# The first weight block of a streaming encoder layer: its two pieces loaded as two halves of 64 rows each, its cast shared by two engines, fewer warming matmuls

## The chip, the cores and the metric

The kernel runs on one core of a Trainium2 chip (trn2). The metric is the device time of one execution in microseconds (us), as the median of several runs. Before the change three runs gave 428.34, 428.74 and 429.11 us, median 428.74. The engines are named as the profile names them: PE (TensorE; PEld is its weight load), ACT (ScalarE), DVE (VectorE), POOL (GpSimd) and SP (SyncE, which here only issues DMAs).

## The reference

One inference step of an encoder layer for 256 prompt frames and 32 sample frames (288 together, `T`), width 1024. What matters here is its first step, one combined input projection of all frames in float32:

```python
def project(x, w_in, b_gates):
    B, T, _ = x.shape
    p = x @ w_in
    cuts = [int(c) for c in np.cumsum(COL_SIZES)[:-1]]
    (qa, ka, va, oa, za, ia, fa, qb, kb, vb, zb, qi, ki, wi, ga, gb) = jnp.split(p, cuts, axis=-1)
...
```

The pieces feed two branches (a gated matrix memory and a sparse attention), whose outputs are gated, projected again by `w_out_a`, `w_out_b` and `w_o`, added to the input and normalised.

## The kernel before

All weights are cut into tiles of 128 output columns by 1024 rows (8 blocks `k` of 128 rows), and a list `ORDER`, written out by hand, sets the order in which PE multiplies them. float32 accuracy is had from three products of a faster type: a weight `w` is split into a high part `wh` (a cast, on ACT) and the rest `wl = w - wh` (a subtraction, on DVE), the input likewise into `xh` and `xl`, and PE adds up `wh*xh`, `wh*xl` and `wl*xh` in PSUM.

For most tiles one DMA brings the whole tile. The first five tiles (`FIRST = 5`) are done in another way, so that PE can start early. The host packs for each of the 8 blocks `k` the block of the input (288 columns) and the block's share of the five tiles (5 x 128 columns) side by side in `in_first`, 928 columns in all (`LEAD`). Each block is loaded into a buffer `lead[k]` (`wst_k` in the trace), split by ACT and DVE, and multiplied for all five tiles at once by `first_products` (L957) into five PSUM banks.

Only block 0 comes in two pieces, the cut being at column 416 (`cut = T + 128`): piece A, the input and tile 0, is loaded from SP's queue (L163), and piece B, tiles 1 to 4, from ACT's queue (L164). SP then issues the DMAs of blocks 1 to 7 (L166). The work on a block is

```python
        act.copy(xh[:, k], raw[:, 0:T])                                              # L171
        if k == 0:
            dve.tensor_copy(wh[:, 0:128], raw[:, T:cut])                             # L173
        dve.tensor_tensor(xl[:, k], raw[:, 0:T], xh[:, k].bitcast(F32), OP.subtract) # L174
```

then, for block 0, `wl` of tile 0 on DVE (L176), and for every block the cast of the other `wh` columns on ACT (L178) and their `wl` on DVE (L179). ACT and DVE work through their instructions in the order written.

PE's first instructions are `WARM = 18` matmuls on a tile of zeros (`warm`, 256 columns, `keep_warm`, L150) whose result nobody reads. Behind them stands `first_products`: for block 0 the three products of tile 0 (288 columns each), then twelve of tiles 1 to 4 (224 columns each); for each later block fifteen products. From L896 to L898 on follow the other tiles. The order of instructions is fixed in the source (a manual schedule); a framework adds the semaphores, and an ACT table load (`ACT_TABLE_LOAD`) ahead of ACT's first operation that needs one.

Of the kernel before, what the change touches and what calls it, by code (L numbers as in the profile page):

```python
# [10 lines left out]
F32 = mybir.dt.float32  # L11
# [3 lines left out]
OP = mybir.AluOpType  # L15
# [7 lines left out]
T = TP + TS  # L23
# [2 lines left out]
BH, BD = 8, 128  # L26
IH, ID = 8, 64
CHUNK = 64
WARM = 18
MID = 4  # L30
FIRST = 5
LEAD = T + 128 * FIRST
# [53 lines left out]
def body(ctx, tc, a, o):  # L86
    nc = tc.nc
    pe, act, dve, pool, sp = nc.tensor, nc.scalar, nc.vector, nc.gpsimd, nc.sync
# [5 lines left out]
    def sb(name, shape, dt=F32, tag=None, bufs=1):  # L94
        return P.tile(shape, dt, name=name, tag=tag or name, bufs=bufs)
# [27 lines left out]
    def pair(name):  # L123
        return (sb(f"wh{name}", [128, KT * 128], F32R, tag="wh", bufs=4),
                sb(f"wl{name}", [128, KT * 128], F32R, tag="wl", bufs=4))
# [16 lines left out]
    xh = sb("xh", [128, KT, T], F32R)  # L142
    xl = sb("xl", [128, KT, T], F32R)
# [4 lines left out]
    def keep_warm(n):  # L148
        for _ in range(n):
            pe.matmul(wp[:, :256], lhsT=warm[:, :128], rhs=warm, start=True, stop=True)  # L150

    keep_warm(WARM)

# [6 lines left out]
    rtab = early2[:8, NREL:2 * NREL]  # L160
    lead = [sb(f"wst_k{k}", [128, KT * 128], tag="wst", bufs=8) for k in range(KT)]
    cut = T + 128
    sp.dma_start(lead[0][:, 0:cut], a["first"][:, 0, 0:cut])  # L163
    act.dma_start(lead[0][:, cut:LEAD], a["first"][:, 0, cut:])  # L164
    for k in range(1, KT):
        sp.dma_start(lead[k][:, 0:LEAD], a["first"][:, k])  # L166
    leads = []
    for k in range(KT):
        raw, (wh, wl) = lead[k], pair(f"_k{k}")
        leads.append((wh, wl))  # L170
        act.copy(xh[:, k], raw[:, 0:T])  # L171
        if k == 0:
            dve.tensor_copy(wh[:, 0:128], raw[:, T:cut])  # L173
        dve.tensor_tensor(xl[:, k], raw[:, 0:T], xh[:, k].bitcast(F32), OP.subtract)  # L174
        if k == 0:
            dve.tensor_tensor(wl[:, 0:128], raw[:, T:cut], wh[:, 0:128].bitcast(F32), OP.subtract)  # L176
        p = cut if k == 0 else T
        act.copy(wh[:, p - T:LEAD - T], raw[:, p:LEAD])  # L178
        dve.tensor_tensor(wl[:, p - T:LEAD - T], raw[:, p:LEAD], wh[:, p - T:LEAD - T].bitcast(F32), OP.subtract)  # L179
    for t in range(FIRST, FIRST + 3):  # L180
        load_tile(t)
# [763 lines left out]
    def out_bank(t):  # L945
        if t < FIRST:
            return bank(f"pj{t}")
        return ps.tile([128, 512], F32, name=f"pj{t}", tag="proj", bufs=2)

    def first_products():  # L950
        p = [out_bank(t) for t in range(FIRST)]
        for k, (wh, wl) in enumerate(leads):
            for tiles in ((0,), (1, 2, 3, 4)) if k == 0 else (range(FIRST),):
                for w, x in ((wh, xh), (wh, xl), (wl, xh)):
                    for t in tiles:
                        new = slice(CHUNK if ORDER[t][0] == "qi" else 0, T)
                        pe.matmul(p[t][:, new], lhsT=w[:, 128 * t:128 * t + 128], rhs=x[:, k, new],  # L957
                                  start=(k == 0 and w is wh and x is xh), stop=(k == KT - 1 and w is wl))
        return p


# [109 lines left out]
    def free_from(i):  # L1071
        n, j = ORDER[i - 8]
        return POS[n, j | 3] if n in ("vb", "va") else 0

    first = first_products()
    for t in (FIRST, FIRST + 1):
        split_hi(t)
# [117 lines left out]
```

## Time and profile before

| | before |
|---|---|
| median of 3 runs | 428.74 us (428.34 to 429.11) |
| the profiled execution, its own time | 429.2 us |
| its span, first to last instruction | 427.1 us |
| PE busy | 420.4 us, 98% of the span |
| first product of real data on PE | 5.07 us |
| end of block 0 on PE | 7.62 us |
| end of block 7 on PE | 19.79 us |

The profiled execution lies 0.46 us above the median, and its span 2.1 us below its own time. Times in the rows below count from the start of the span. A busy PE is not a PE at its full pace, since matmuls overlap: the start of one matmul to the start of the next is what one costs.

### The profile page before, as it was taken

To read this page: it belongs to the slowest core of one execution; us is meant where nothing else is said; L and a number is where in the kernel's file an instruction comes from. 1 tells how busy PE (TensorE), PEld (TensorE's weight loads), DVE (VectorE), ACT (ScalarE), POOL (GpSimd) and SP (SyncE) were. 2 spreads that over 40 slices of the span, in tenths; PEclk is the share of its full clock that TensorE was granted. 3 is DMA by queue.
4 is the path that set the end of the run, shared out by engine and by line. 5 is a ranking of instruction groups with operands and counts; after the bars stand their busy time and mean duration, and the time that the engine had idled before them with its cause. 6 is when DMAs were issued, how large, how long until landed. Compare 5 with 4: busy or idle time off the path is not lost.

```text
span 427.1 us, 8153 instructions
## 1 busy us (share of the span) xinstructions
PE 420.4 (98%) x3189; PEld 395.6 (93%) x3189; DVE 299.0 (70%) x601; ACT 226.7 (53%) x443; POOL 22.6 (5%) x41
## 2 busy tenths in 40 slices
PE   8999999999999999999999999999999999999994
PEld 7999999878999998789999999999999999998874
DVE  5669989986756665665999987876454465665674
ACT  6776445425666666458795465555434444446402
POOL 0000000000400000000001101101000000000031
PEclk9999999999999999999999999999999999999999
DMA  8987869575945630349544456545555658543014
GB/s 305 362 319 206 294 204 309 214 198 204 411 156 147 218 122 0 114 141 335 152 148 150 109 171 215 148 148 151 168 178 155 176 163 265 153 137 124 27 46 140
DMA packets 29746, 78.81 MB, mean 185 GB/s; under 512 B 8548, under 2 KB 11852, under 8 KB 28908
## 3 DMA queue, kind: packets, MB, share of 16 engines
q1 hardware_dynamic: 28844, 76.98, 56.0%
q10 hardware_dynamic: 864, 1.32, 0.9%
q8 instruction: 25, 0.41, 0.4%
q14 instruction: 13, 0.11, 0.1%
HBM read 72.52 MB, written 7.67 MB: 188 GB/s over the span
## 4 chain that ended last, share of the span: by engine, by line
PE 96%; DVE 1%; ACT 1%; POOLq 0%; issue 0%; DVEq 0%; ACTq 0%
PE pj L896 22%; PE pj L897 22%; PE pj L898 21%; PE yn L938 5%; PE pj L957 3%; PE pj L912 2%; PE pj L914 2%; PE pj L913 2%; PE warm_p L150 1%; PE vap L912 1%; PE vbp L912 1%; PE vbp L914 1%; PE vap L920 1%; PE vbp L920 1%; PE vap L914 1%; PE vbp L913 1%
## 5 line engine op out<-in xcount | busy, mean ns | idle before, releaser
L132 ACT CAST wh<-wst 128x1024 fp32r<-128x1024 f32 x112 | 117.8, 1052 | 137.5 <-PE pj L897 64.8
L896 PE MATMUL pj<-xh,wh 128*128 128x288 f32 x576 | 171.7, 298 | 0.1
L897 PE MATMUL pj<-xl,wh 128*128 128x288 f32 x576 | 169.9, 295 | 0.0
L898 PE MATMUL pj<-xh,wl 128*128 128x288 f32 x576 | 169.8, 295 | 0.0
L139 DVE TENSOR_TENSOR wl<-wst,wh 128x1024 fp32r<-128x1024 f32 x112 | 136.3, 1219 | 32.2 <-ACT wh L132 31.9
L896 PEld LDWEIGHTS pj<-xh,wh 128*128 128x128 f32 x576 | 108.3, 188 | 1.8 <-issue 0.4
L897 PEld LDWEIGHTS pj<-xl,wh 128*128 128x128 f32 x576 | 108.3, 188 | 0.1
L898 PEld LDWEIGHTS pj<-xh,wl 128*128 128x128 f32 x576 | 108.3, 188 | 0.0
L896 PE MATMUL pj<-bbh,wh 128*128 128x288 f32 x64 | 18.9, 295 | 0.0
L897 PE MATMUL pj<-bal,wh 128*128 128x288 f32 x64 | 18.9, 295 | 0.0
L898 PE MATMUL pj<-bah,wl 128*128 128x288 f32 x64 | 18.9, 295 | 0.0
L897 PE MATMUL pj<-bbl,wh 128*128 128x288 f32 x64 | 18.9, 295 | 0.0
L898 PE MATMUL pj<-bbh,wl 128*128 128x288 f32 x64 | 18.8, 294 | 0.0
L896 PE MATMUL pj<-bah,wh 128*128 128x288 f32 x64 | 18.8, 293 | 0.0
L912 PE MATMUL pj<-wh,xh 128*128 128x512 f32 x32 | 13.0, 405 | 0.0
L938 PE MATMUL yn<-wh,mxh 128*128 128x512 f32 x32 | 12.9, 404 | 0.0
L938 PE MATMUL yn<-wl,mxh 128*128 128x512 f32 x32 | 12.7, 397 | 0.1
L913 PE MATMUL pj<-wl,xh 128*128 128x512 f32 x32 | 12.6, 394 | 0.0
L914 PE MATMUL pj<-wh,xl 128*128 128x512 f32 x32 | 12.6, 394 | 0.0
L938 PE MATMUL yn<-wh,mxl 128*128 128x512 f32 x32 | 12.6, 394 | 0.0
L896 PEld LDWEIGHTS pj<-bbh,wh 128*128 128x128 f32 x64 | 12.1, 188 | 0.0
L896 PEld LDWEIGHTS pj<-bah,wh 128*128 128x128 f32 x64 | 12.0, 188 | 0.0
(490 smaller groups left out, 672.2 us busy)
## 6 DMA issues: line engine op xcount, KB each, us to landing
wst<-in_w SPq DMA_DIRECT2D x112, 512.0 KB, 4.0
wst_k<-in_first SPq DMA_DIRECT2D x7, 464.0 KB, 5.0
rscr<-rrow SPq DMA_DIRECT2D x2, 768.0 KB
out_k<-kbT SPq DMA_DIRECT2D x1, 1152.0 KB
stC<-in_state_C SPq DMA_DIRECT2D x1, 1028.0 KB, 5.9
out_C_sample<-stC SPq DMA_DIRECT2D x1, 1028.0 KB
bm<-rscr SPq DMA_DIRECT2D x1, 1024.0 KB
ckT<-in_cache_k SPq DMA_DIRECT2D x1, 1024.0 KB
```

The source lines that it names most:

```text
L132: act.copy(split[t][0], stage[t])
L139: dve.tensor_tensor(wl, stage[t], wh.bitcast(F32), OP.subtract)
L150: pe.matmul(wp[:, :256], lhsT=warm[:, :128], rhs=warm, start=True, stop=True)
L896: pe.matmul(p[:, :T], lhsT=wh[:, c], rhs=h[:, k], start=(k == 0), stop=False)
L897: pe.matmul(p[:, :T], lhsT=wh[:, c], rhs=l[:, k], start=False, stop=False)
L898: pe.matmul(p[:, :T], lhsT=wl[:, c], rhs=h[:, k], start=False, stop=(k == KT - 1))
L912: pe.matmul(banks[i], lhsT=xh[:, k, r], rhs=wh[:, c], start=(k == 0), stop=False)
L913: pe.matmul(banks[i], lhsT=xh[:, k, r], rhs=wl[:, c], start=False, stop=False)
L914: pe.matmul(banks[i], lhsT=xl[:, k, r], rhs=wh[:, c], start=False, stop=(k == KT - 1))
L920: pe.matmul(banks[4][32 * i:32 * i + 32, 0:256].rearrange("p (g c) -> p g c", g=g), lhsT=xs0[:, kk], rhs=w[:, i], start=(kk == 0), stop=(k ...
L938: pe.matmul(p, lhsT=x[:, k, r], rhs=w[:, c], start=first and i == 0, stop=last and i == 2)
L957: pe.matmul(p[t][:, new], lhsT=w[:, 128 * t:128 * t + 128], rhs=x[:, k, new], start=(k == 0 and w is wh and x is xh), stop=(k == KT - 1 an ...
```

## The change

- Piece A and piece B of block 0 are each loaded as two DMAs of 64 rows: SP issues rows 0 to 63 of A and then of B, ACT rows 64 to 127 of A and then of B. The byte count is the same.
- On DVE, `wl` of tile 0 stands ahead of `xl`.
- The 512 columns of `wh` of tiles 1 to 4 of block 0 are cast half by ACT (256 columns) and half by DVE (256 columns).
- The warming matmuls ahead of the first product go from 18 to 13, and one more stands behind each of the first two kinds of product of tile 0, whose order becomes `wh*xh`, `wl*xh`, `wh*xl`.

```diff
-WARM = 18
+WARM = 13
...
-    sp.dma_start(lead[0][:, 0:cut], a["first"][:, 0, 0:cut])
-    act.dma_start(lead[0][:, cut:LEAD], a["first"][:, 0, cut:])
+    for c in (slice(0, cut), slice(cut, LEAD)):
+        for q, r in ((sp, slice(0, 64)), (act, slice(64, 128))):
+            q.dma_start(lead[0][r, c], a["first"][r, 0, c])
     for k in range(1, KT):
         sp.dma_start(lead[k][:, 0:LEAD], a["first"][:, k])
...
         act.copy(xh[:, k], raw[:, 0:T])
         if k == 0:
             dve.tensor_copy(wh[:, 0:128], raw[:, T:cut])
+            dve.tensor_tensor(wl[:, 0:128], raw[:, T:cut], wh[:, 0:128].bitcast(F32), OP.subtract)
         dve.tensor_tensor(xl[:, k], raw[:, 0:T], xh[:, k].bitcast(F32), OP.subtract)
-        if k == 0:
-            dve.tensor_tensor(wl[:, 0:128], raw[:, T:cut], wh[:, 0:128].bitcast(F32), OP.subtract)
         p = cut if k == 0 else T
-        act.copy(wh[:, p - T:LEAD - T], raw[:, p:LEAD])
+        q = LEAD - 256 if k == 0 else LEAD
+        act.copy(wh[:, p - T:q - T], raw[:, p:q])
+        if q < LEAD:
+            dve.tensor_copy(wh[:, q - T:LEAD - T], raw[:, q:LEAD])
         dve.tensor_tensor(wl[:, p - T:LEAD - T], raw[:, p:LEAD], wh[:, p - T:LEAD - T].bitcast(F32), OP.subtract)
...
         for k, (wh, wl) in enumerate(leads):
             for tiles in ((0,), (1, 2, 3, 4)) if k == 0 else (range(FIRST),):
-                for w, x in ((wh, xh), (wh, xl), (wl, xh)):
+                for w, x in ((wh, xh), (wl, xh), (wh, xl)) if len(tiles) == 1 else ((wh, xh), (wh, xl), (wl, xh)):
                     for t in tiles:
                         new = slice(CHUNK if ORDER[t][0] == "qi" else 0, T)
                         pe.matmul(p[t][:, new], lhsT=w[:, 128 * t:128 * t + 128], rhs=x[:, k, new],
                                   start=(k == 0 and w is wh and x is xh), stop=(k == KT - 1 and w is wl))
+                    if len(tiles) == 1 and w is not wl:
+                        keep_warm(1)
```

How this moves instructions is shown at two places, from the built programs. A row's bracket names the semaphores that are waited for ahead of it: the engines' own names count instructions of that engine, and each `DMAHW` number is one transfer's completion. What waits for two semaphores has a semaphore instruction of its own in front of it, on the same engine.

The first place is the start of ACT's program. Before, with piece B's DMA first and piece A's completion being DMAHW1:

```order
L164 DMA wst_k_90<-in_first 128x512
L171 ACT_TABLE_LOAD
L171 CAST xh<-wst_k_90 128x288 [waits DMAHW1_49]
L178 CAST wh_k_107<-wst_k_90 128x512 [waits DMAHW0_49]
L171 CAST xh<-wst_k_91 128x288 [waits DMAHW2_49]
```

Now, with the completions of A's halves being DMAHW1 (SP's half) and DMAHW0 (ACT's half), and those of B's DMAHW3 and DMAHW2:

```order
L165 DMA wst_k_85<-in_first 64x416
L165 DMA wst_k_85<-in_first 64x512
L172 ACT_TABLE_LOAD [waits DMAHW1_49]
L172 CAST xh<-wst_k_85 128x288 [waits DMAHW0_49]
L179 CAST wh_k_104<-wst_k_85 128x256 [waits DMAHW3_49,DMAHW2_49]
L172 CAST xh<-wst_k_86 128x288 [waits DMAHW4_49]
```

The cast of `xh` now needs two transfers, and the extra semaphore wait stands ahead of the table load, where before the table load stood free of any wait.

The second place is PE, from the last warming matmul to the first product of tiles 1 to 4. Before:

```order
L150 MATMUL warm_p<-warm 128x256
L957 MATMUL pj_199<-xh,wh_k_107 128x288 [waits DVE_49,Activation_49]
L957 MATMUL pj_199<-xl,wh_k_107 128x288 [waits DVE_49]
L957 MATMUL pj_199<-xh,wl_k_108 128x288 [waits DVE_49]
L957 MATMUL pj_200<-xh,wh_k_107 128x224 [waits Activation_49]
```

Now:

```order
L960 MATMUL pj_197<-xh,wh_k_104 128x288 [waits DVE_49,Activation_49]
L150 LDWEIGHTS warm
L150 MATMUL warm_p<-warm 128x256
L960 MATMUL pj_197<-xh,wl_k_105 128x288 [waits DVE_49]
L960 MATMUL pj_197<-xl,wh_k_104 128x288 [waits DVE_49]
L150 LDWEIGHTS warm
L150 MATMUL warm_p<-warm 128x256
L960 MATMUL pj_198<-xh,wh_k_104 128x224 [waits Activation_49]
```

Five warming matmuls fewer stand ahead of the first product, and one each behind the first and the third.

## Rows read from the trace of the kernel before

**Rows 1.** Page, part 1 (busy time by engine) and part 4 (chain, by engine).

```profile
PE 420.4 (98%) x3189; PEld 395.6 (93%) x3189; DVE 299.0 (70%) x601; ACT 226.7 (53%) x443; POOL 22.6 (5%) x41
...
PE 96%; DVE 1%; ACT 1%; POOLq 0%; issue 0%; DVEq 0%; ACTq 0%
```

**Rows 2.** Chain of waits in order of time, start: start us, us, what.

```profile
5.15 14.80 PE pj L957 x120
```

**Rows 3.** Timeline, first 8 us: start us, us, engine, line, operation, out<-in, count.

```profile
0.80 0.41 ACTq L164 DMA_DIRECT2D wst_k<-in_first  x1
0.81 0.39 SPq L163 DMA_DIRECT2D wst_k<-in_first  x1
...
1.12 4.02 PE L150 MATMUL warm_p<-warm 128*128 128x256 bf16 x18 [1.12 <-DVE warm L145]
1.24 1.28 ACT L171 ACT_TABLE_LOAD   x1 [1.24 <-PEq L1173]
...
4.59 0.43 ACT L171 CAST xh<-wst_k 128x288 fp32r<-128x288 f32 x1 [2.06 <-DMA wst_k<-in_first]
...
4.93 0.61 ACT L178 CAST wh_k<-wst_k 128x512 fp32r<-128x512 f32 x1
5.05 0.46 DVE L174 TENSOR_TENSOR xl<-wst_k,xh 128x288 fp32r<-128x288 f32 x1 [0.24 <-ACT xh L171]
...
5.07 0.61 PE L957 MATMUL pj<-xh,wh_k 128*128 128x288 f32 x1
5.57 0.61 PE L957 MATMUL pj<-xl,wh_k 128*128 128x288 f32 x1
5.63 0.68 DVE L179 TENSOR_TENSOR wl_k<-wst_k,wh_k 128x512 fp32r<-128x512 f32 x1
...
5.87 0.43 ACT L171 CAST xh<-wst_k 128x288 fp32r<-128x288 f32 x1 [0.33 <-DMA wst_k<-in_first]
5.97 0.44 PE L957 MATMUL pj<-xh,wl_k 128*128 128x288 f32 x1
...
6.21 0.68 PE L957 MATMUL pj<-xh,wh_k 128*128 128x224 f32 x4
6.21 0.72 ACT L178 CAST wh_k<-wst_k 128x640 fp32r<-128x640 f32 x1
6.34 0.46 DVE L174 TENSOR_TENSOR xl<-wst_k,xh 128x288 fp32r<-128x288 f32 x1
...
6.73 0.61 PE L957 MATMUL pj<-xl,wh_k 128*128 128x224 f32 x4
6.97 0.83 DVE L179 TENSOR_TENSOR wl_k<-wst_k,wh_k 128x640 fp32r<-128x640 f32 x1 [0.17 <-ACT wh_k L178]
...
7.17 0.61 PE L957 MATMUL pj<-xh,wl_k 128*128 128x224 f32 x4
```

**Rows 4.** DMA queues (packets, MB, share): both queues to 3.0 us, SP's to 3.6.

```profile
q1 hardware_dynamic: 67, 0.11, 19.6%
q10 hardware_dynamic: 44, 0.09, 15.2%
...
q1 hardware_dynamic: 122, 0.20, 23.6%
```

**Rows 5.** Instructions of line 178: name, count, ns min/median/max, first and last start.

```profile
L178 ACTq EVENT_SEMAPHORE  x4: 17/17/17, 9.5 to 13.1; - x4
```

**Rows 6.** Timeline of ACT around 198 us, its only other table load.

```profile
197.33 1.05 ACT L132 CAST wh<-wst 128x1024 fp32r<-128x1024 f32 x1
198.40 1.28 ACT L842 ACT_TABLE_LOAD   x1
199.69 0.41 ACT L842 ACTIVATE sg<-pj 128x288 f32<-128x288 f32 x1
```

**Rows 7.** Windows, blocks 1 and 7 on PE: us, PE busy, granted clock, DMA.

```profile
7.62:9.36 1.74, 1.74 (x17) 1.00 1.04 399
...
18.05:19.79 1.74, 1.74 (x18) 1.00 0.99 314
```

## The prediction

> **What bounds the kernel now.** I read the page first: PE is busy for 420.4 of 427.1 us, and the chain that ended last is PE for 96% [rows 1]. Followed in order of time, the chain is one unbroken run of L957 products from 5.15 us [rows 2], and the products of the other tiles behind it. So the time is, to a first approximation, the moment when PE starts on real data, plus the pace that it then keeps. Whatever moves the end of block 0 on PE moves the end of the kernel by as much, as long as ACT and DVE stay ahead of PE in the later blocks.
>
> Then the timeline of the first 8 us [rows 3]. Piece A is issued at 0.81 us on SP's queue and piece B at 0.80 on ACT's. ACT loads its table from 1.24 to 2.52 and then idles for 2.06 us until A has landed; the cast of `xh` starts at 4.59. The first product follows 0.48 us later, at 5.07. PE warms from 1.12 to 5.14, right up to that product. Block 0 then ends at 7.62, where the first stretch of [rows 7] begins; from there each block takes 1.74 us, the first and the last of the seven alike.
>
> The pace of PE has to be read from the starts of matmuls. The granted clock reads 1.00 in every window [rows 7], but a product of 288 columns takes 0.24 us at 5.97 (to the next start at 6.21), which is 1.2 GHz, and the 18 warming ones take 4.02 us, 0.22 each for 256 columns, the same level. From 6.73 to 7.17 four products of 224 columns take 0.44 us, 0.11 each: the upper level, 2.4 GHz. The four before, 6.21 to 6.73, take 0.52, that is 0.19 for the first and 0.11 for the others. So the clock rose at about 6.35 us, after 5.2 us of work with almost no break, and it had not risen after the 4.0 us of warming alone.
>
> **The change part by part.** The sum is made against the profiled execution, 429.2 us, which lies 0.46 above the median of 428.74; what it gives is then added to that median.
>
> *The halves.* Before, the two queues share the DMA engines about evenly: by 3.0 us SP's queue (q1) has moved 0.11 MB and ACT's (q10) 0.09, together 0.20; q1 alone reaches 0.20 only by 3.6 [rows 4]. Piece A is 128 x 1664 B = 0.21 MB. When both queues carry A first, it is through when both together have moved that much, 0.6 us sooner: A lands at 3.99 instead of 4.59. Bounds: no gain (the halves get in each other's way) and 0.6. I take 0.6, because it is the order of the bytes that changes, and the rows show both queues being served side by side. The Trainium skill, page "DMA: Bandwidth & Descriptors", section "Rules for kernel authors", says of two transfers to disjoint partition halves not to bother, since both spray over the same 16 engines and serialize; by that rule alone A would still land at 4.59. The trace shows why it may not hold here: the second half takes the place of B, not of idle engines. The rule stands below as a rival.
>
> *The table load.* The cast of `xh` now needs two completions. The first stands in a semaphore instruction of its own, as the four two-wait casts of L178 already have [rows 5], and the built order puts it ahead of the table load. The load, hidden in idle time before, now starts only when SP's half of A has landed: 3.99 + 0.02 to 5.29, since a load takes 1.28 both at 1.24 and at 198.40 [rows 3, 6]. The cast starts at 5.30 instead of 4.59, 0.71 late, and the first product at 5.78 instead of 5.07. Between load and next operation I count 0.01 us, as after the load at 198.40 (198.40 + 1.28 to 199.69 [rows 6]). The Trainium skill, page "ScalarE: Activation LUTs", section "What ACT_TABLE_LOAD costs", adds a drain of about 1.38 us to each 1.28 us load. By it the cast would start at 6.68; no such gap stands in the rows at 198 us, so the sum goes without it.
>
> *The order in block 0.* From 5.78, if the clock rises at 6.35 as before: the first product to the next start 0.40 (as 5.57 to 5.97), 6.18; a warming matmul 0.21, 6.39; then `wl`, ready for long since DVE no longer puts it behind `xl`, and `xl` (its subtraction starts 0.46 after the cast of `xh`, at 5.76, and PE follows 0.52 later, 6.28), 0.13 each, 6.65; a warming matmul 0.11, 6.76; twelve products at 0.11, 1.32, so 8.08. Before it was 7.62: **+0.46**. The moved cast costs nothing on this path: ACT's 256 columns end by about 6.1, DVE's by about 6.5 and their `wl` (0.68) by about 7.2, while PE reaches that `wl` eight products after 6.76, at 7.64. If that cover fails, it is DVE that is late, by tenths.
>
> *Later blocks.* ACT's cast of block 1 starts at 5.95 for 5.87, since that data lands no sooner; DVE is about 0.7 late (block 1's `xl` at 7.05 for 6.34, `wl` done by 8.4), and PE, at block 1 from 8.08, asks for them at 8.7 and 9.2. DVE needs 1.2 us a block for PE's 1.74, so it catches up. The extra DMAs (one on each queue) delay SP's issue of block 1 by some 0.4 us; block 1 is used at 5.87, bound by the bytes ahead of it, and those are the same. Zero.
>
> *The clock.* This is the unknown. Thirteen warming matmuls end at 4.02 - 5 x 0.21 + 1.12 = 4.1 us. Then PE idles until 5.78, 1.7 us in which before it worked. At the earliest the clock rises at 6.35 as before; at the latest as long after the restart as it took from the first matmul before, 5.78 + 5.2 = 11.0. At the lower level a block of three products of 288 columns and twelve of 224 takes 3 x 0.24 + 12 x 0.187 = 2.96 us for 1.74, so each microsecond by which the rise is late costs 1 - 1.74/2.96 = 0.41 us. The bounds are 0 and 4.65 x 0.41 = 1.9. I take the middle, a rise at 8.7: 2.35 x 0.41 = **+0.96**, because neither row is nearer: 3 us of warming before the gap did not raise the clock, and 1.1 us of work behind it will hardly do so by 6.35.
>
> Sum: 0.46 + 0.96 = +1.4 us. On the median, 428.74 + 1.4 = **430.1 us**; on the profiled execution 430.6.
>
> **The rivals.**
> 1. *The clock rises as before*, by 6.4: only +0.46 is left, 429.2. For it: PE has worked for 3 us before the gap and works again from 5.78. Against it: 4.0 us unbroken were not enough before.
> 2. *The table load does not wait* (the semaphore is passed before it, or the load runs beside it). Then the cast starts at 4.0 and the first product at 4.5, and this ends on the other side. But block 1 cannot start on PE before ACT has cast its `wh`, 6.21 + 0.72 = 6.93 [rows 3], and that hangs on block 1's landing. So block 0 ends at 7.0 at best: -0.6, 428.1. This decides if the load's end comes before A lands. Against it: the built order.
> 3. *Halving buys nothing*: A lands at 4.59, the cast starts at 5.90, and all of the above comes 0.6 later, 430.7. The two halves then share the engines and push nothing ahead. This is what the rule on halves of the Trainium skill (page "DMA: Bandwidth & Descriptors") would make of it.
> 4. *ACT pauses behind the load* when it comes this late: the rows before cannot exclude it for this first load, behind which ACT idled for 2.06 us anyway. With a pause as long as the load (1.3 us) the gap on PE is 3.0 us, and with the same clock term the time is 431.4; a later clock gives 432.4. The drain that the Trainium skill states (page "ScalarE: Activation LUTs") would be such a pause.
>
> **How the numbers follow.** Forecast 0.53, rival 1 0.30, rival 2 0.05, rival 3 0.07, rival 4 0.05. A measurement of this kernel tells about 0.2% (0.86 us) from no change: faster means below 427.9, slower above 429.6. Rival 2 ends within that bound, so faster gets 0.04 for what I have not seen. Slower is rivals 3 and 4 and nearly all of the forecast (unless the clock rises before 7.3), 0.60; the rest, 0.36, is the same. The range takes rival 1 less some scatter at the bottom, 428.9, and a clock that rises at 11.0 at the top, 428.74 + 0.46 + 1.9 = 431.1; outside are rivals 2 and 4 and the edges, about 0.18. The forecast's own range is 429.6 to 431.1.
>
> **What would show it.** In the new profile ACT's first table load should start near 4.0 and not near 1.6 (after its two DMA issues), the cast of `xh` near 5.3, and the first product near 5.8, behind 1.7 us of idle PE. A load at 1.6 means rival 2; a load at 4.6, rival 3; a gap of over 1 us behind it, rival 4. Four products of 224 columns in 0.75 us instead of 0.44 after 6.8 show the late clock; if they take 0.44, rival 1 holds. From block 2 on each block should take 1.74 us again, and the end should lie as far behind the end of block 7 as before. If the difference arose after block 7, all of this would be wrong.

## The result and the profile after

| | before | after |
|---|---|---|
| median of the comparison | 428.47 us (428.22 to 429.11, 9 runs) | **430.88 us** (429.39 to 432.67, 9 runs) |
| ratio after to before | | 1.0054, 95% interval 1.0035 to 1.0074 |
| the profiled execution, its own time | 429.2 us | 431.41 us |
| its span | 427.1 us | 429.4 us |
| first product of real data on PE | 5.07 us | 5.14 us |
| end of the first five tiles on PE | 19.95 us | 22.53 us |
| from there to the end of the span | 407.15 us | 406.87 us |

The change makes the kernel slower by about 2.4 us. The forecast was +1.4, and 430.88 lies inside its range. The last three lines of the table tell where to look. The first product is not late. The end of the first five tiles is late by 2.58 us, and the rest of the kernel takes as long as before. So all of the loss arises between 5.1 and 22.5 us.

The page's part 4 of the changed kernel, which answers to the second line of [rows 1]:

```profile
PE 94%; DVE 1%; DMA 1%; ACT 1%; POOLq 0%; issue 0%; DVEq 0%; ACTq 0%
```

DMA now stands in the chain with 1%. The chain in order of time says which transfer that is (start us, us, what); it answers to [rows 2]:

```profile
0.81 0.58 ACTq L165
1.42 5.25 DMA wst_k<-in_first
6.69 0.41 ACT wh_k L179
7.15 15.38 PE pj L960 x117
```

Before, the unbroken run of products began at 5.15 us. Now it begins at 7.15, with the last twelve products of block 0 (117 products in the row are these and the 105 of blocks 1 to 7), and what it waited for is the transfer that ACT's queue issued at 1.42 us. That is ACT's half of piece B, which landed at 6.67. This is the surprise: the forecast looked at piece A and at the table load.

The timeline of the first 9 us (start us, us, engine, line, operation, out<-in, count, and in brackets idle time before it and what ended it), which answers to [rows 3]:

```profile
0.80 1.22 SPq L165 DMA_DIRECT2D wst_k<-in_first  x2
0.81 1.48 ACTq L165 DMA_DIRECT2D wst_k<-in_first  x2
...
2.06 4.96 SPq L167 DMA_DIRECT2D wst_k<-in_first  x7
3.37 1.28 ACT L172 ACT_TABLE_LOAD   x1 [3.37 <-DMA wst_k<-in_first]
3.71 0.23 DVE L174 CAST wh_k<-wst_k 128x128 fp32r<-128x128 f32 x1 [2.65 <-DMA wst_k<-in_first]
...
4.66 0.43 ACT L172 CAST xh<-wst_k 128x288 fp32r<-128x288 f32 x1
...
5.14 0.40 PE L960 MATMUL pj<-xh,wh_k 128*128 128x288 f32 x1 [1.07 <-ACT xh L172]
...
5.38 0.28 PE L150 MATMUL warm_p<-warm 128*128 128x256 bf16 x1
...
6.69 0.41 ACT L179 CAST wh_k<-wst_k 128x256 fp32r<-128x256 f32 x1 [1.60 <-DMA wst_k<-in_first]
...
7.15 0.70 PE L960 MATMUL pj<-xh,wh_k 128*128 128x224 f32 x4 [0.99 <-ACT wh_k L179]
...
7.62 0.43 ACT L172 CAST xh<-wst_k 128x288 fp32r<-128x288 f32 x1 [0.52 <-DMA wst_k<-in_first]
...
7.69 0.83 PE L960 MATMUL pj<-xl,wh_k 128*128 128x224 f32 x4
8.32 1.05 PE L960 MATMUL pj<-xh,wl_k 128*128 128x224 f32 x4
```

The table load does wait for SP's half of A, as forecast, but that half is there by 3.37 us, and ACT's half by 3.71. The load ends at 3.37 + 1.28 = 4.65, and the cast of `xh` starts at 4.66, only 0.07 us later than before. PE idles twice: 1.07 us ahead of the first product, which warming covered before, and 0.99 us ahead of tiles 1 to 4, because B's casts start at 6.69, where before ACT's started at 4.93. Block 1's input is cast at 7.62 instead of 5.87.

The windows of the same stretch (window, us, then per engine the busy time and count, the granted clock, DMA share, GB/s):

```profile
7.15:7.93 0.78, 0.78 (x7) 0.78 (x8) 0.68 (x1) 0.31 (x1) 0.00 (x0) 1.00 1.00 395
7.93:9.17 1.24, 1.24 (x8) 1.24 (x7) 0.92 (x2) 1.12 (x4) 0.00 (x0) 0.50 1.02 398
9.17:11.34 2.17, 2.17 (x11) 2.17 (x11) 2.11 (x5) 1.87 (x5) 0.00 (x0) 0.50 1.03 397
11.34:13.10 1.76, 1.76 (x18) 1.76 (x16) 1.76 (x4) 1.62 (x4) 0.00 (x0) 1.00 1.02 391
```

Behind the two gaps the granted clock is 0.50 from 7.93 to 11.34 us, that is 1.2 GHz. The products say the same: four of 224 columns take 0.54 us from 7.15 and 0.85 from 8.32 (to block 1 at 9.17). Before, the clock had risen for good at about 6.35.

Ahead of 7.15 the column is no help, since it reads 1.00 also where PE works at the lower pace (the warming before, for one). The products tell: the first product of tile 0 takes 0.40 us here, for 0.61 before [rows 3], and the warming matmul behind it 0.28, for 0.44 in e4 below, whose clock was low there. So in this execution the clock was up before the first product, in spite of the gap ahead of it. The trace's own record of the clock's changes says so too: up at 4.51 us, down at 7.92, up for good at 11.34. Before it has one rise, at 6.37.

With these rows the 2.58 us can be added up along PE. First product: +0.07. Tile 0 with its two warming matmuls, 5.14 to 6.17, against 5.07 to 6.21: −0.11. Gap before tiles 1 to 4: +0.98. Their twelve products, 7.15 to 9.17, against 6.21 to 7.62: +0.61. Block 1, 9.17 to 11.94, against 1.74: +1.03. After that nothing more is lost. The last two are for the most part the clock: 1.64, where the prediction's factor gives 3.41 us at the lower level x 0.41 = 1.40.

This is one execution. The mean granted clock is 0.994 in it and in one other of the nine (431.04 us), and 0.996 to 1.000 in the other seven, so a fall like this one probably stands in two of the nine. What the clock did in the others is seen only in the profiles of related kernels below.

**Why B was late.** One row of before's timeline and the shares of the two queues from 3.2 to 4.0 us, first of before (queue: packets, MB, share of 16 engines):

```profile
1.26 3.82 SPq L166 DMA_DIRECT2D wst_k<-in_first  x7
...
q1 hardware_dynamic: 85, 0.18, 58.4%
q10 hardware_dynamic: 75, 0.13, 44.6%
```

then of the changed kernel from 3.2 to 4.0 us, and its ACT queue from 5.6 to 6.4:

```profile
q1 hardware_dynamic: 37, 0.06, 46.9%
q10 hardware_dynamic: 16, 0.03, 38.7%
...
q10 hardware_dynamic: 2, 0.00, 0.7%
```

Just behind A the engines are busy for 86% of the stretch but move 53 packets instead of 160, 113 GB/s instead of 379. A packet takes 0.86 x 16 x 0.8 / 53 = 0.21 us of an engine where before it took 0.08, at about the same mean size (1.7 and 1.9 KB). ACT's half of B still has two packets to move after 5.6 us. B is usable only when the last of them is in. The issues are slower too: two DMAs of 64 rows take 1.22 us on SP's queue and 1.48 on ACT's, 0.6 to 0.7 each on the mean (0.57 to 0.87), where one of 128 rows took 0.4, so SP issues blocks 1 to 7 from 2.06 us instead of 1.26.

B's landing is not the same in every execution. Six profiles have the same four half transfers. In the three where ACT's two issues took longer than SP's (the change, e3, e7: 1.31 to 1.49 us for 1.21 to 1.22) B's first cast starts at 6.5 to 7.1 us; in the three where SP's took longer (e1, e5, e9: 1.47 to 1.48 for 1.20) it starts at 5.3 to 5.9. Block 1 is late in all six (6.8 to 7.7, for 5.87 before). What sets the order is not shown.

### The profile page after: what moved, and what is told of

The parts are those of the page before. It is cut to its first block, busy times and chain, and to the rows that moved or that the text cites. A ratio compares the mean times of both kernels' runs of the same rounds, so it can differ in the third digit from the quotient of the medians.

```text
span 429.4 us, 8154 instructions
## 1 busy us (share of the span) xinstructions
PE 420.9 (98%) x3186; PEld 396.2 (92%) x3186; DVE 300.3 (70%) x602; ACT 226.5 (53%) x443; POOL 22.5 (5%) x41
## 4 chain that ended last, share of the span: by engine, by line
PE 94%; DVE 1%; DMA 1%; ACT 1%; POOLq 0%; issue 0%; DVEq 0%; ACTq 0%
PE pj L899 22%; PE pj L900 21%; PE pj L901 21%; PE yn L941 5%; PE pj L960 4%; PE pj L915 2%; PE pj L916 2%; PE pj L917 2%; DMA wst_k<-in_first 1%; PE vap L915 1%; PE vbp L915 1%; PE vbp L917 1%; PE vap L923 1%; PE vbp L923 1%; PE vap L917 1%; PE vbp L916 1%
## 5 line engine op out<-in xcount | busy, mean ns | idle before, releaser
L899 PE MATMUL pj<-xh,wh 128*128 128x288 f32 x576 | 171.7, 298 | 0.1
```

The costliest lines, as they stand in the source:

```text
L899: pe.matmul(p[:, :T], lhsT=wh[:, c], rhs=h[:, k], start=(k == 0), stop=False)
```

## The experiments

Each was run against the kernel before on the same chip. Theory after the result: data lands late because of the halves, and the gaps in PE that come of it and of the fewer warming matmuls cost the clock. Rival: the wait of the table load is the cost. Column "end" is the end of the first five tiles on PE, taken from the chain (before 19.95, changed kernel 22.53). It is that of one execution, and moves with the clock's rise in it.

| run | what | median, us | before, us | ratio (95%) | end, us |
|---|---|---|---|---|---|
| e1_table_early | change, table load first, by a new tile | 432.13 | 428.83 | 1.0079 (1.0061 to 1.0096) | 21.54 |
| e7_table_early_again | the same without the new tile | 430.41 | 428.75 | 1.0034 (1.0023 to 1.0045) | 23.68 |
| e11_tile_only | before, with the new tile alone | 431.08 | 428.65 | 1.0050 (1.0034 to 1.0065) | 19.87 |
| e2_b_whole | change, B in one DMA | 431.00 | 428.83 | 1.0051 (1.0039 to 1.0063) | 22.28 |
| e5_halves_only | before, with the halves alone | 429.94 | 428.75 | 1.0034 (1.0019 to 1.0050) | 20.91 |
| e6_a_whole_b_behind | before, A and B whole on SP's queue | 429.96 | 428.75 | 1.0030 (1.0018 to 1.0042) | 21.04 |
| e4_warming_only | before, with the new warming alone | 430.37 | 428.83 | 1.0033 (1.0021 to 1.0045) | 21.27 |
| e3_warm18 | change, with 18 + 2 warming matmuls | 430.07 | 428.83 | 1.0028 (1.0017 to 1.0040) | 21.35 |
| e9_always_warm | change, with 18 + 1 + 1 + 8 | 430.18 | 428.75 | 1.0038 (1.0025 to 1.0051) | 21.16 |
| e10_casts_only | before, with the casts and orders alone | 428.25 | 428.65 | 0.9994 (0.9985 to 1.0003) | 19.23 |
| e8_b_after_table | before, table load first, B issued behind it | 428.31 | 428.65 | 0.9994 (0.9985 to 1.0003) | 19.62 |
| e12_both | e10 and e8 together | 428.39 | 428.79 | 0.9996 (0.9987 to 1.0005) | 19.03 |

### The table load: e1, e11, e7

e1 takes the load from behind the wait: a one-column copy into a new tile stands on ACT right behind its two DMA issues, and the load goes with it.

```diff
+    tbl = sb("tbl", [128, 1], BF)
+    act.copy(tbl, warm[:, 0:1])
     for k in range(1, KT):
```

> The change, with a one-column copy on ACT behind its two DMA issues, so that the table load stands ahead of the wait and not behind it. Theory 'the table load is the cost' (the prediction's): the cast of xh starts where both halves of A have landed, near 3.7 us instead of 4.66, the first product near 4.2 instead of 5.14, and the time falls by 0.7 to 0.9 us, to about 430.0. Theory 'piece B is the cost': B's casts still start at 6.7, block 0 ends no earlier than in the changed kernel (9.17, or 8.5 with the clock up), PE idles longer ahead of B, and the time is that of the change, 430.9 within 0.5, or worse by the clock.

The load moved and the first product came at 4.33 us. The first five tiles ended at 21.54, 0.99 earlier than with the change; but B was early in this profile (its cast at 5.30), so that isn't the load's doing alone. Yet the kernel took 432.13 us, longer than the change: from there to the end of the span it took 408.9 us instead of 406.9. That was in no theory, and e11 puts only the tile into the kernel before:

```diff
+    tbl = sb("tbl", [128, 1], BF)
+    pool.memset(tbl, 0.0)
```

> The kernel before with nothing but one more tile of 2 bytes per partition, written once by GpSimd, allocated ahead of the tiles of wh and wl, as in e1_table_early. Theory 'where the tiles lie in SBUF sets the pace of the products': the stretch from block 7 to the end is about 2 us longer and the time is 430.5 to 431. Rival 'e1_table_early was slower for another reason': within 0.3 us of 428.75.

It costs 2.4 us, as much as the whole change, and not at the start (first five tiles at 19.87, 0.08 earlier). In the groups of instructions by line (line, engine, operation, out<-in, count, busy us, mean ns) first of the kernel before and then of e11, this is one group of products:

```profile
L896 PE MATMUL pj<-xh,wh 128*128 128x288 f32 x576 | 171.7, 298 | 0.1
```

```profile
L898 PE MATMUL pj<-xh,wh 128*128 128x288 f32 x576 | 172.7, 300 | 0.0
```

These products take 0.6% longer, those of the two lines behind 0.4 and 0.7%. So the time of e1 says nothing on the load. e7 repeats it without a tile, by copying one column into a part of `xh` that is overwritten later:

```diff
+    act.copy(xh[:, KT - 1, 0:1], warm[:, 0:1])
     for k in range(1, KT):
```

> The change with the table load ahead of the wait, as in e1_table_early, but without a new tile: the one-column copy writes a column of xh that is written again later. In e1_table_early every stretch of the kernel ran 0.4% slower to the end, which the table load can't explain. If the new tile of 2 bytes per partition (all later tiles shifted by it) made that, the distance from the end of block 7 to the end of the span is that of the change here (407.0 us, not 409.0). Then the table load's own price shows: theory 'it costs what it delays' 0.7 to 0.9 us less than the change, 430.0 to 430.2; theory 'the data of tiles 1 to 4 and of block 1 come later anyway' within 0.5 us of the change, 430.9.

Its profile, timeline of ACT and PE:

```profile
2.33 1.28 ACT L166 ACT_TABLE_LOAD   x1 [2.33 <-issue]
...
4.21 0.61 PE L961 MATMUL pj<-xh,wh_k 128*128 128x288 f32 x1
...
6.95 1.20 PE L961 MATMUL pj<-xh,wh_k 128*128 128x224 f32 x4 [1.17 <-ACT wh_k L180]
...
10.74 1.29 PE L961 MATMUL pj<-xl,wh_k 128*128 128x288 f32 x5
```

The first product came 0.93 us earlier than with the change, and PE then stood 1.17 us before tiles 1 to 4, since B landed about as late as there. Five products of 288 columns still took 1.10 us from 10.74 to the next group (0.58 at the upper level), so the clock was still low (the trace records its rise at 13.25); this profile is the slowest of its ten runs (428.98 to 432.36). The median, 430.41, can't be told from the change's 430.88 by the intervals. So the wait of the table load is not the whole cause: with the load early the kernel is still 0.34% slower than before. A price of its own is neither shown nor excluded: e7 lies 0.5 us under the change by the medians and 0.9 by the ratios, as much as the load delays. In the profiles of the change and e7 PE waits for B in any case, so the earlier product gains nothing. In those of e2 and e9 below, where B came in time, the load stands in the chain and the first product is late by it (5.78 and 5.54, for 5.07 before).

### The halves: e2, e5, e6

e2 keeps A in halves and loads B with one DMA on ACT's queue:

```diff
-    for c in (slice(0, cut), slice(cut, LEAD)):
-        for q, r in ((sp, slice(0, 64)), (act, slice(64, 128))):
-            q.dma_start(lead[0][r, c], a["first"][r, 0, c])
+    for q, r in ((sp, slice(0, 64)), (act, slice(64, 128))):
+        q.dma_start(lead[0][r, 0:cut], a["first"][r, 0, 0:cut])
+    act.dma_start(lead[0][:, cut:LEAD], a["first"][:, 0, cut:])
```

> The change, with piece B again in one DMA of 128 rows on ACT's queue, behind ACT's half of A. Theory 'B's halves are late because they are halves' (small transfers on two queues, the last of them sharing an engine with block 1): B lands near 5 us, block 1 near 6, PE's gap ahead of the products of tiles 1 to 4 shrinks from 1.0 us to under 0.4, and the time falls by 1 us or more, under 430. Theory 'any second transfer behind A's halves starts late': B lands after 6 us again and the time stays within 0.5 us of 430.9.

The timeline of ACT and PE in e2:

```profile
4.00 1.28 ACT L172 ACT_TABLE_LOAD   x1 [4.00 <-DMA wst_k<-in_first]
...
5.29 0.43 ACT L172 CAST xh<-wst_k 128x288 fp32r<-128x288 f32 x1
5.63 0.40 ACT L179 CAST wh_k<-wst_k 128x256 fp32r<-128x256 f32 x1
5.78 0.61 PE L960 MATMUL pj<-xh,wh_k 128*128 128x288 f32 x1 [1.70 <-ACT xh L172]
...
7.50 0.43 ACT L172 CAST xh<-wst_k 128x288 fp32r<-128x288 f32 x1 [1.47 <-DMA wst_k<-in_first]
```

B is no longer late: ACT goes on to its cast at 5.63 without a wait. This run is the forecast's own start, number for number (load at 4.00, cast at 5.29, first product at 5.78 behind 1.70 us of idle PE). But the time, 431.00, is that of the change. B's halves are not the whole cause. Block 1 is still late (7.50), but its weights are cast by 8.56 and PE asks for them only at 9.68, so in this profile nothing is lost by that. What is lost is the later start and the late clock, whose rise the trace records at 10.25.

e5 puts the halves alone into the kernel before: its 18 warming matmuls, its casts and orders stay.

```diff
-    sp.dma_start(lead[0][:, 0:cut], a["first"][:, 0, 0:cut])
-    act.dma_start(lead[0][:, cut:LEAD], a["first"][:, 0, cut:])
+    for c in (slice(0, cut), slice(cut, LEAD)):
+        for q, r in ((sp, slice(0, 64)), (act, slice(64, 128))):
+            q.dma_start(lead[0][r, c], a["first"][r, 0, c])
```

> The kernel before with the DMAs of the change alone: A and B as halves of 64 rows; 18 warming matmuls, casts and products as before. Theory 'the halves starve the DMA engines' (four issues of 0.57 to 0.87 us in place of two of 0.4, and the bytes per second fall to 50 to 140 GB/s between 3.2 and 4.0 us): B lands after 6 us and block 1 near 7.6, so the time rises by 1.0 to 1.5 us over 428.8, most of what the change with 18 warming matmuls lost (430.07). Rival 'the cast sharing or the order on DVE makes the data late': the time stays within 0.4 us of before.

It costs 1.2 us (429.94 for 428.75; 1.5 by the ratio), with the clock up early (recorded rise at 4.58) and eleven runs spread from 428.86 to 433.07. The table load waits here too, so the first product comes at 5.54. In the profile's timeline blocks 1 and 2 are both late: block 1's weights are cast by 8.02 and PE takes them at 8.08, so little of the late start is lost by itself, and PE then waits for block 2 until 10.23.

```profile
6.96 0.43 ACT L172 CAST xh<-wst_k 128x288 fp32r<-128x288 f32 x1 [0.44 <-DMA wst_k<-in_first]
...
9.12 0.43 ACT L172 CAST xh<-wst_k 128x288 fp32r<-128x288 f32 x1 [1.09 <-DMA wst_k<-in_first]
```

e6 asks whether it is the halves, or that both queues put A first. It issues A whole and B whole behind it on SP's queue, and nothing on ACT's:

```diff
-    act.dma_start(lead[0][:, cut:LEAD], a["first"][:, 0, cut:])
+    sp.dma_start(lead[0][:, cut:LEAD], a["first"][:, 0, cut:])
```

> The kernel before with piece B's DMA moved from ACT's queue to SP's, behind piece A, both whole (128 rows). If what brings A early is only that B's bytes no longer run beside it, A lands by 4.0 us here too, without any halving, and the issues stay at 0.4 us: the first product near 4.6, B near 4.9, block 1 near 6.2, time 0.2 to 0.6 us under before. If one queue alone ramps up more slowly than two, A lands at 4.4 or later and the time is that of before or up to 0.5 us worse.

The timeline of ACT in e6:

```profile
3.44 0.43 ACT L171 CAST xh<-wst_k 128x288 fp32r<-128x288 f32 x1 [1.36 <-DMA wst_k<-in_first]
...
4.04 0.62 ACT L178 CAST wh_k<-wst_k 128x512 fp32r<-128x512 f32 x1 [0.17 <-DMA wst_k<-in_first]
...
7.52 0.43 ACT L171 CAST xh<-wst_k 128x288 fp32r<-128x288 f32 x1 [2.86 <-DMA wst_k<-in_first]
```

A is there at 3.44 and B at 4.04, the earliest of all, without a half. So what brought A forward in the change is that it goes ahead of B, not that it is cut. But block 1 comes at 7.52, and the kernel is 1.2 us slower than before, which neither expectation had. From 4.0 to 4.8 us SP's queue reads (packets, MB, share of 16 engines), first in the kernel before and then in e6

```profile
q1 hardware_dynamic: 92, 0.33, 102.3%
...
q1 hardware_dynamic: 54, 0.20, 103.7%
```

The engines are as busy, but move 0.20 MB for 0.33, with packets of about the same size (3.7 and 3.6 KB): 0.25 us of an engine per packet for 0.14. It is a slow stretch as in the change, weaker (251 GB/s, where the change fell to 113) and one step later. So the lateness is not one of halves as such: it comes too with whole pieces, if all stand on one queue. What in the DMA engines makes the packets slow there stays open.

### The clock: e4, e3, e9

e4 puts the change's warming alone into the kernel before (13 matmuls, one each behind the first two kinds of product of tile 0):

```diff
-WARM = 18
+WARM = 13
...
+                    if len(tiles) == 1 and w is not wl:
+                        keep_warm(1)
```

> The kernel before with the warming alone changed: 13 matmuls ahead, one each behind the first two products of tile 0; the DMAs, the casts and the order of the products are as before. A lands at 4.6 and the first product starts at 5.07, so PE idles for 1.0 us from 4.07. Theory 'the gaps cost through the clock': the median rises by 0.5 to 1.5 us over 428.5 and the spread grows beyond 1 us. Theory 'a gap of 1 us does nothing by itself, the late data is the cost': within 0.3 us of 428.5.

The timeline of PE and ACT in e4:

```profile
4.89 0.61 PE L957 MATMUL pj<-xh,wh_k 128*128 128x288 f32 x1 [0.81 <-ACT xh L171]
5.30 0.44 PE L150 MATMUL warm_p<-warm 128*128 128x256 bf16 x1
...
5.67 0.43 ACT L171 CAST xh<-wst_k 128x288 fp32r<-128x288 f32 x1 [0.31 <-DMA wst_k<-in_first]
...
6.27 1.03 PE L957 MATMUL pj<-xh,wh_k 128*128 128x224 f32 x4
...
8.80 0.88 PE L957 MATMUL pj<-xh,wh_k 128*128 128x288 f32 x5
```

All data is as early as before, or 0.2 earlier. What differs is PE's work: none for 0.81 us ahead of the first product, and two warming matmuls behind it. The twelve products of 224 columns then take 2.53 us instead of 1.41: the clock rises near 9 us, not at 6.35. The median is 1.5 us longer, at the upper end of what the first theory expected; the spread, 0.75 us, did not grow. The gap and the two warming matmuls come together here, but e3 below has the two as well and keeps its clock.

e3 gives the changed kernel its 18 warming matmuls back, the two between staying:

```diff
-WARM = 13
+WARM = 18
```

> The change with 18 warming matmuls ahead instead of 13. They end at 5.1 us, where the first product starts in the changed kernel, so the first gap on PE is gone and the products are no later. Theory 'the gaps let the clock fall or rise late': the clock is up before block 0 ends, the times lose their spread of 3 us, and the median falls by about 1 us, to 429.5 to 430. Theory 'the gap ahead of B alone does it': the median stays within 0.4 us of 430.9 and the spread stays.

The timeline of PE in e3:

```profile
7.59 0.70 PE L960 MATMUL pj<-xh,wh_k 128*128 128x224 f32 x4 [1.17 <-ACT wh_k L179]
8.13 0.61 PE L960 MATMUL pj<-xl,wh_k 128*128 128x224 f32 x4
```

The clock is up when tiles 1 to 4 start and stays up: four products take 0.54 and then 0.45 us, where the change ended with 0.85. The median is 430.07, so of the change's 2.4 us some 1.1 can be put down to the clock (by the ratios, 1.0054 less 1.0028 of 428.6 us; the intervals just overlap). B landed late here as well, at 7.11, and PE waited 1.17 us for it.

e9 also puts warming matmuls into the second gap, so that PE has work all the time:

```diff
-WARM = 13
+WARM = 18
...
-                    if len(tiles) == 1 and w is not wl:
-                        keep_warm(1)
+                    if len(tiles) == 1:
+                        keep_warm(1 if x is xh else 8)
```

> The change with 18 warming matmuls ahead and eight more behind the third product of tile 0 (and one behind each of the others), so that PE has work in both gaps: up to the first product and until B has been cast. The data come as late as in the change. Theory 'the lost time is late data plus a clock that is late or falls for the gaps': the clock rises by 6.5 us and stays, block 0 ends near 8.6 and the times lie close together, at 429.6 to 430.1; what is left over before is the late data, about 1 us. Rival 'the clock follows the real products and not the warming': no better than 430.9.

The timeline of ACT and PE in e9:

```profile
5.39 0.40 ACT L179 CAST wh_k<-wst_k 128x256 fp32r<-128x256 f32 x1
...
7.42 0.69 PE L960 MATMUL pj<-xh,wh_k 128*128 128x224 f32 x4
```

The clock held, and it was no faster than e3, 430.18 (0.7 us less than the change by the ratios): the eight matmuls keep tiles 1 to 4 waiting (7.42) though B was there early this time, its cast at 5.39 following ACT's cast of `xh` at once. With the same DMAs B's casts stood at 6.69 in the change, 7.13 in e3 and 5.39 here. The change's nine runs spread over 3.3 us where before's spread over 0.9, which fits such a scatter of the landing and of the clock. What is left with the clock held, 1.2 us in e3, is what the halves cost alone in e5 (1.2). The 1.4 of e9 is no second witness: behind its first product (5.54, late by the table load) PE waits for no data up to block 1 at 8.83, and the warming matmuls in the way make up the rest.

### What is left of the change, and a better way: e10, e8, e12

e10 keeps of the change only DVE's order, the shared cast and the order of tile 0's products; the DMAs and the warming are those of before.

```diff
-    for c in (slice(0, cut), slice(cut, LEAD)):
-        for q, r in ((sp, slice(0, 64)), (act, slice(64, 128))):
-            q.dma_start(lead[0][r, c], a["first"][r, 0, c])
+    sp.dma_start(lead[0][:, 0:cut], a["first"][:, 0, 0:cut])
+    act.dma_start(lead[0][:, cut:LEAD], a["first"][:, 0, cut:])
...
-WARM = 13
+WARM = 18
...
-                    if len(tiles) == 1 and w is not wl:
-                        keep_warm(1)
```

> The kernel before with the third part of the change alone: wl of tile 0 ahead of xl on DVE and in the products, and the 512-column cast shared, 256 on ACT and 256 on DVE; DMAs and the 18 warming matmuls as before. The prediction priced this at nothing. Theory: the products of tiles 1 to 4 start within 0.2 us of 6.21, time within 0.3 us of 428.75. Rival 'DVE becomes late': 0.3 to 0.8 us slower.

The five tiles end at 19.23, 0.72 earlier in the profile, but the medians differ by 0.4 us and the interval holds no change. The profiles flatter it: that of before lies 0.46 us above its median, e10's is the fastest of its eleven runs, A was used at 4.37 in it for 4.59 with the same DMAs, and its clock rose at 5.33 instead of 6.37, which by the factor 0.41 is worth 0.4. The products of tiles 1 to 4 start at 5.58, earlier than the 6.21 within 0.2 that was expected, for the same reasons. The shared cast did no harm.

e8 gets A early in another way. In the program ACT's table load stands before everything and B's issue behind it, so that A, whole on SP's queue, is issued ahead of B:

```diff
     sp.dma_start(lead[0][:, 0:cut], a["first"][:, 0, 0:cut])
+    act.copy(xh[:, KT - 1, 0:1], warm[:, 0:1])
     act.dma_start(lead[0][:, cut:LEAD], a["first"][:, 0, cut:])
```

> The kernel before with the table load first on ACT and piece B's DMA, whole and on ACT's queue, issued behind it (near 2.3 us instead of 0.8); A whole and blocks 1 to 7 on SP's queue as before. Here A needn't share with B, and block 1 stands right behind A, so that the DMA engines never run out of work. Theory 'in every run that brought A early the engines ran dry behind A and B, and that made block 1 late': A lands by 4.0, no dip below 250 GB/s after 2.8 us, block 1 near 6 as before, B near 5.2; time 0 to 0.5 us under before (18 warming matmuls hold the first product at 4.9). Rival 'whatever lets A through early slows the start of the others': block 1 lands after 6.7 and the time is 0.8 us or more above before.

The timeline of ACT and its queue in e8:

```profile
1.10 0.42 ACTq L165 DMA_DIRECT2D wst_k<-in_first  x1
...
3.47 0.43 ACT L172 CAST xh<-wst_k 128x288 fp32r<-128x288 f32 x1 [1.18 <-DMA wst_k<-in_first]
...
4.24 0.62 ACT L179 CAST wh_k<-wst_k 128x512 fp32r<-128x512 f32 x1 [0.33 <-DMA wst_k<-in_first]
...
5.43 0.43 ACT L172 CAST xh<-wst_k 128x288 fp32r<-128x288 f32 x1 [0.58 <-DMA wst_k<-in_first]
...
7.82 0.43 ACT L172 CAST xh<-wst_k 128x288 fp32r<-128x288 f32 x1 [1.33 <-DMA wst_k<-in_first]
```

Against what was expected, B's issue did not wait for the load's end (0.81 + 1.28 = 2.09): it stands at 1.10, only 0.3 us later than before. That was enough. A, B and block 1 are all used earlier than before (3.47 for 4.59, 4.24 for 4.93, 5.43 for 5.87); block 2 is later (7.82 for 7.07), at no cost that PE shows. In its stretch from 3.2 to 4.0 us the two queues moved 0.29 MB (362 GB/s), nearly as much as before. PE makes no use of it, since the 18 warming matmuls hold it until 4.8. The time is that of before.

e12 joins e8 and e10:

> The two things that did no harm, together: piece A whole on SP's queue, ACT's table load before everything and piece B whole behind it on ACT's queue, and the shared cast with the new order of DVE and of tile 0's products; 18 warming matmuls ahead of the first product, none between. Theory (the start is bound by when PE is let go, by the data of block 1, and by the clock): A used near 3.5 us, first product at 4.8 (held by the 18 warming matmuls), clock risen near 5.5 to 6.0, block 0 ends near 6.9, since block 1 is there by 5.5 and its weights are cast by 6.7; block 7 ends near 19.1, 0.7 earlier than before; 427.9 to 428.1 us against 428.6, ratio 0.998 to 0.999, about what five rounds can tell. Rival (block 1's cast becomes the bound, ACT being late): block 0 takes 2.4 us or more, with PE idle before block 1, and no gain over the table change or the casts alone (428.3). Rival (late clock as in the change): block 7 ends past 20 us, 429.5 or more.

The five tiles end 0.92 earlier in the profile, at 19.03 (the fastest of its eleven runs, with the clock's rise at 5.00), and the median is 428.39 for 428.79, ratio 0.9996 (0.9987 to 1.0005). Of the ratio expected, 0.998 to 0.999, the lower end lies outside that. No version beats the kernel before by more than its measurement can tell. What would be left to take is the time between A (3.4) and the first product (4.8), but e4 shows what less warming can cost.

## Why the prediction was right

The direction, the size within the range, and the place (block 0 and block 1, carried unchanged to the end) held. Inside, the terms came out otherwise, and one that was put at zero was not, so that the closeness of the number is in part luck.

1. *The halves, A at 3.99 instead of 4.59.* Right in sign, too small in the change's profile: 3.37 and 3.71; in e2 it is 4.00 and 4.03. The reason, that both queues put A first, holds: e6 has A whole at 3.44 when it goes ahead of B. The rule of the Trainium skill, page "DMA: Bandwidth & Descriptors", section "Rules for kernel authors", not to bother with two transfers to disjoint partition halves, is borne out by e6 in that sense, that the cutting itself gains nothing. Rival 3, which made it mean that A lands no earlier, falls.
2. *The table load waits for SP's half*, +0.71. The mechanism is as forecast: the load starts with that landing, takes 1.28, and the cast follows 0.01 us behind its end, so rival 4 falls. The drain that the Trainium skill states (page "ScalarE: Activation LUTs", section "What ACT_TABLE_LOAD costs") does not show in these traces. Rival 2 falls too: the load does not run ahead. The size hangs on when A lands: +0.07 in the change's profile, +0.70 in e2, where A landed at 4.00.
3. *"The extra DMAs ... Zero"* is the term that failed. It counted bytes only: "that data lands no sooner", and so also no later. In the profile B was late by 1.8 us and block 1 by 1.75 (7.62 for 5.87). The issues of SP came 0.8 later, not 0.4, and the engines' packets took 0.21 us for 0.08 behind A. e5 prices the halves, with the wait of the load that they bring: 1.2 us.
4. *The clock*, +0.96, taken in the middle of a wide range. A late rise behind the gap is what e4 shows (near 9 us, where nothing else is late) and e2 (10.25, where 8.7 was forecast). e2 is the forecast's own case but for B in one piece, and with its rise the forecast's sum is 0.46 + 3.9 x 0.41 = +2.1, for 2.2 measured. In the profile of the change itself the clock did something that the forecast had not thought of: it was up before the first product and fell behind the second gap, which term 3 denied. That it costs 1.4 to 1.6 there, not far from the forecast, is luck. By the ratios of e9 and e3 the clock is 0.7 to 1.1 of 2.4, with intervals that overlap the change's. One reason given for the middle was misread: from 5.78 to 6.35 is 0.57 us of work, not 1.1.
5. *The order in block 0 and the moved cast.* The +0.46 held a start 0.71 late, so the order itself was put at -0.25. Tile 0's stretch shows -0.11, with the clock up, which it was not before, so the order's own share can't be read from it. That the moved cast costs nothing is borne out by e10.

So the forecast came within 0.8 us because the table load cost less than forecast and the late data more. The parts do not add up either: the warming alone costs 1.5 and the halves alone 1.2, together 2.4 and not 2.7. That the late data and the late clock partly fall into the same microseconds would explain it, but the difference is also within the scatter.

## What to carry to other kernels

At the start of a kernel, count for each transfer what lies ahead of it on its queue and when its last packet comes, not only the bytes: bringing one piece forward by putting it on two queues made the next two late, while delaying the competing transfer by 0.3 us (e8) brought the first three forward and made only the fourth later, where PE did not feel it. Here the warming matmuls had to reach to the first product: with 0.8 us without work there the kernel was 1.5 us longer (e4). Work that waits at the next place anyway gains nothing from an earlier start (e7). And read more than one profile of a start: B's landing and the clock's rise each moved by 1.8 us between executions with the same transfers, or the same warming matmuls, ahead of them.

## What the runs showed of the hardware that was not expected

- One tile of 2 bytes per partition, laid out ahead of the weight buffers, makes the products of the three lines with 576 each 0.4 to 0.7% longer (172.7 us for 171.7 at the first) and the kernel 2.4 us (e11). The tile and its one memset are the only edit; that it is the new place of the buffers behind it that counts is argued, not shown.
- A DMA issue took 0.39 to 0.41 us as the first of its queue before, but 0.57 to 0.87 with 64 rows, and a whole one behind such a half 0.60 as well (e2, on ACT's queue from 1.42 us).
- DMA engines can be shown busy and move little: 113 GB/s at 86% busy from 3.2 to 4.0 us in the change, for 379 before, and 251 GB/s at 104% from 4.0 to 4.8 in e6, for 416 before. It followed the halves (change) and two whole pieces on one queue (e6), and did not follow one whole piece on each queue (before; e8, 362 and 418). Why is open.
- With the same 18 warming matmuls from 1.12 us on, the recorded rise of the clock lies between 4.58 us (e5, before the warming ends) and 6.37 (before). With 13 of them it came at 9.08 (e4), 10.09 (e1), 10.25 (e2) and 13.25 (e7), and at 4.51 in the change, while PE stood idle.
- The clock, once up, fell at 7.92 in the change, behind a second gap of 0.98 us (the first was 1.07), and stayed low to 11.34. In e3 it did not fall behind a gap of 1.17 us.
